# A max-pooling kernel with two input buffers: a half-length second load, and a shorter load near the end

## The chip, the core and the metric

The kernel runs on one core of one Trainium2 chip. Its time is the device time of one execution, in microseconds (us). Before the change the median of three runs is 335.14 us (334.92 to 335.22).

## What is computed

The input is a float32 array of 32 x 256 rows of 4096 numbers. Each row is cut into 256 windows of 16 numbers, and the output holds the maximum of each window:

```python
batch, channels, length = 32, 256, 4096
output_size = 256
...
for i in range(output_size):
    start = int(i * length / output_size)
    end = int((i + 1) * length / output_size)
    result[:, :, i] = np.max(x[:, :, start:end], axis=-1)
```

That is 134.2 MB read, 8.4 MB written, and one maximum over each 16 numbers.

## The kernel before

**Tiling.** All windows are spread over the 128 partitions, 16384 windows for each. A window takes 64 bytes of a partition, so a load of n windows brings n x 64 bytes into each partition as one row: 1024 windows are rows of 64 KB and 8 MB in all. The windows come in two groups, each laid out in memory as 128 long rows: group a with 13424 windows a partition, group b with 2960. Group a is walked from its end to its start, group b forwards.

**Loads.** The first load has 128 windows (8 KB rows), then come twelve of 1024, one of 1008, two of 1024, and a last one of 912. In this text the loads behind the first are named by the loop's counter, `n_loads` in the kernel before and `k` in the kernel after: k0, k1 and so on. Before the change, k0 to k11 have 1024 windows, k12 has 1008, k13 and k14 have 1024 and k15 has 912. All loads are issued by SyncE (SP) in this order, on one queue: L87 for the first, L96 for the rest. SP issues one after the other and waits at each until its buffer is free.

**Buffers.** One tile, `ring`, holds two buffers of 1024 + 152 windows. Even loads go to the lower, odd loads to the upper. Within its buffer a load lies at offset 0 or, for every second pair of loads (`moved`), at offset 152. VectorE (DVE) reduces every load in two instructions (L56): first the part that the next load in this buffer will overwrite (872 of 1024 windows), then the 152 windows that it won't touch. So load k+2 is issued as soon as the larger part of load k is reduced, beside the reduction of the smaller. The first load lies in the 152-window end of the lower buffer, and is out of the way of k0 and k1.

**Results.** They are collected in the tile `kept`. At the end the results of the last load, which lie in `ring`, are stored from ScalarE's queue (L114), and those of group a and of the rest of group b from SP's queue, behind the last load (L117).

Nothing else computes. TensorE, ScalarE and GpSimd have no work beyond that store and four constants.

Of the kernel before, what the change touches and what calls it, by code (L numbers as in the profile page):

```python
# [1 line left out]

# [4 lines left out]


@with_exitstack
def kernel(  # L10
    ctx: ExitStack,
    tc: tile.TileContext,
    x: bass.AP,
    output_size: bass.AP,
    out: bass.AP,
):

    nc = tc.nc
    P = nc.NUM_PARTITIONS
    fp32 = mybir.dt.float32

    B, C, L = x.shape
    O = int(output_size)  # L30
    assert L % O == 0, (L, O)
    W = L // O
    total = B * C * O // P
    assert B * C * O % P == 0

    CHUNK = 1024
    GAP = 152
    FIRST = 128
    LOADS_A, LOADS_B = 13, 2

    LESS = 16
    group_a = [FIRST] + [CHUNK] * (LOADS_A - 1) + [CHUNK - LESS]
    last = total - sum(group_a) - LOADS_B * CHUNK
    group_b = [CHUNK] * LOADS_B + [last]
    assert 0 < last and last * (W + 1) <= CHUNK * W

    pool = ctx.enter_context(tc.tile_pool(name="pool", bufs=1))
    ring = pool.tile([P, 2 * (CHUNK + GAP) * W], fp32, tag="ring", name="ring")
    kept = pool.tile([P, total - last], fp32, tag="kept", name="kept")

    xw = x.flatten_outer_dims().rearrange("r (o w) -> (r o) w", w=W)
    ow = out.flatten_outer_dims().rearrange("r o -> (r o)")

    def pooled(dst, at, n):

        nc.vector.reduce_max(  # L56
            out=dst,
            in_=ring[:, at * W : (at + n) * W].rearrange("p (n w) -> p n w", w=W),
            axis=mybir.AxisListType.X,
        )  # L60

    taken = 0

    def group(n):

        nonlocal taken
        span = slice(taken * P, (taken + n) * P)
        taken += n
        return (
            xw[span].rearrange("(p n) w -> p (n w)", p=P),  # L70
            ow[span].rearrange("(p n) -> p n", p=P),
        )

    stores = []
    n_loads = 0
    base = 0
    for g, loads in enumerate((group_a, group_b)):
        xg, og = group(sum(loads))
        a = sum(loads) if g == 0 else 0
        for n in loads:  # L80
            if g == 0:
                a -= n
            xn = xg[:, a * W : (a + n) * W]
            dst = kept[:, base + a : base + a + n] if n != last else None
            if n == FIRST:

                nc.sync.dma_start(  # L87
                    out=ring[:, CHUNK * W : (CHUNK + n) * W], in_=xn
                )
                pooled(dst, CHUNK, n)  # L90
            else:

                low = n_loads % 2 * (CHUNK + GAP)
                moved = n_loads // 2 % 2
                at = low + moved * GAP
                nc.sync.dma_start(out=ring[:, at * W : (at + n) * W], in_=xn)  # L96
                if n != last:
                    cut = CHUNK - GAP if moved else GAP
                    parts = [(0, cut), (cut, n)]
                    for u, v in parts if moved else parts[::-1]:  # L100
                        pooled(dst[:, u:v], at + u, v - u)
                else:
                    end = (at + CHUNK) * W
                    last_kept = ring[:, end - n : end]
                    pooled(last_kept, at, n)
                n_loads += 1
            if g:
                a += n
        full = a - last if g else sum(loads)
        stores.append((og[:, 0:full], kept[:, base : base + full]))  # L110
        base += full
    assert taken == total

    nc.scalar.dma_start(out=og[:, full : full + last], in_=last_kept)  # L114
    tc.no_sync_barrier()
    for dst, src in stores:
        nc.sync.dma_start(out=dst, in_=src)  # L117


# [1 line left out]
_INS = ['x', 'output_size']  # L121
_OUTS = [((32, 256, 256), 'float32')]

_NUMBERS = {'output_size': 256}


# [26 lines left out]
```

## Time and profile before

| | |
|---|---|
| median of three runs | 335.14 us (334.92 to 335.22) |
| span of the profiled execution, first to last instruction | 333.3 us |
| median above that span | 1.8 us |
| DVE busy | 276.6 us, 32 instructions |
| reduction of 872 windows | 14,686 ns each, 14 of them |
| reduction of 152 windows | 2676 ns each, 15 of them |
| reduction of the first load's 128 windows | 2286 ns |
| reduction of the last 912 windows | 15,353 ns |
| a full load, from issue to landing | 24.0 us, 14 of them in one median |
| first load of 1 MB, from issue to landing | 5.0 us |
| moved by DMA in all | 142.61 MB, 428 GB/s over the span |

The profile is that of one execution; what is known of its time is its span. The 1.8 us lie outside of first and last instruction. The profile's page gives the share of the span in which each engine is busy, the load on the DMA engines in 40 slices, the chain of work that ended last, and the costliest groups of instructions. In a table of stretches, each row is a stretch of time with the busy time of each engine, the granted TensorE clock (which nothing here uses), the mean busy share of the 16 DMA engines, and what they moved. DMA packets are booked at their end, so a stretch of a few us can show a share above 1. In the timeline a row is an instruction or a run of them: start, length, engine, line, and in brackets how long the engine had been idle and for what it waited. "SPq" is an instruction that issues a DMA.

### The profile page before, as it was taken

What the parts mean: (1) busy time and instruction counts of PE and PEld (TensorE: products, weight loads), DVE (VectorE), ACT (ScalarE), POOL (GpSimd) and SP (SyncE); (2) the same over time, 40 slices, a digit from 0 to 9 for tenths busy, and PEclk for the clock granted to TensorE, in tenths of its full rate; (3) what the DMA queues carried; (4) which work ended last, traced back from release to release, by engine and by line L of the source; (5) the groups of instructions that cost most, each with busy time, mean ns of one, the idle gap of its engine ahead of it and who ended that gap; (6) DMA issues with size and microseconds to landing.
All of it is one profiled execution on the core that took longest, in us unless ns stands there. A gap on an engine that the chain in (4) does not pass through costs nothing.

```text
span 333.3 us, 113 instructions
## 1 busy us (share of the span) xinstructions
DVE 276.6 (83%) x32; POOL 0.2 (0%) x4
## 2 busy tenths in 40 slices
DVE  2009979797997979799797979979797988979994
POOL 0000000000000000000000000000000000000000
DMA  9898989999898989999898989999898989899996
GB/s 377 377 503 377 503 377 488 393 425 456 377 503 377 503 377 488 393 448 433 377 503 377 503 377 488 393 456 425 389 480 381 495 377 503 377 462 448 421 412 285
DMA packets 2880, 142.61 MB, mean 428 GB/s; under 512 B 320, under 2 KB 320, under 8 KB 448
## 3 DMA queue, kind: packets, MB, share of 16 engines
q1 hardware_dynamic: 2736, 142.14, 98.7%
q10 hardware_dynamic: 144, 0.47, 0.3%
HBM read 134.22 MB, written 8.39 MB: 428 GB/s over the span
## 4 chain that ended last, share of the span: by engine, by line
DMA 57%; DVE 41%; issue 0%; SPq 0%
DMA ring<-in_x_dram 57%; DVE kept L56 36%; DVE ring L56 5%; SPq L87 0%
## 5 line engine op out<-in xcount | busy, mean ns | idle before, releaser
L56 DVE TENSOR_REDUCE kept<-ring 128x152 f32<-128x2432 f32 (+3 forms) x31 | 261.2, 8466 | 51.8 <-DMA ring<-in_x_dram 51.8
L56 DVE TENSOR_REDUCE ring<-ring 128x912 f32<-128x14592 f32 x1 | 15.4, 15353 | 0.1
L134 POOL MEMSET const-bfloat16-1.0<- 128x1 bf16 x1 | 0.1, 101 | 0.0
L134 POOL MEMSET const-uint8-127<- 128x1 uint8 x1 | 0.1, 101 | 0.0
L134 POOL MEMSET const-float32-0.0<- 128x1 f32 x1 | 0.1, 98 | 0.2 <-issue 0.2
L134 POOL MEMSET const-float32-1.0<- 128x1 f32 x1 | 0.1, 98 | 0.0
## 6 DMA issues: line engine op xcount, KB each, us to landing
ring<-in_x_dram SPq DMA_DIRECT2D x1, 8064.0 KB, 23.7
ring<-in_x_dram SPq DMA_DIRECT2D x1, 7296.0 KB, 21.9
out_dram<-kept SPq DMA_DIRECT2D x1, 6712.0 KB, 37.4
ring<-in_x_dram SPq DMA_DIRECT2D x1, 1024.0 KB, 5.0
out_dram<-kept SPq DMA_DIRECT2D x1, 1024.0 KB, 18.3
out_dram<-ring ACTq DMA_DIRECT2D x1, 456.0 KB, 4.0
ring<-in_x_dram SPq DMA_DIRECT2D x14, 24.0
```

The lines of the kernel that those rows point to most:

```text
L56: nc.vector.reduce_max(out=dst, in_=ring[:, at * W : (at + n) * W].rearrange("p (n w) -> p n w", w=W), axis=mybir.AxisListType.X,)
L134: nc = _bacc.Bacc("TRN2", target_bir_lowering=False, num_devices=1)
```

## The change

The load sizes become

```
before:  128,      12 x 1024, 1008, 2 x 1024, 912
after:   128, 512, 12 x 1024,  496, 2 x 1024, 912
```

A load of 512 windows (32 KB rows, 4 MB) goes between the first load and the first full one, and the load of 1008 windows becomes one of 496. The groups keep their sizes, and so do the stores. There is one load more: k0 has 512 windows, k1 to k12 have 1024, k13 has 496, k14 and k15 have 1024, k16 has 912. Each full load therefore stands one place later in the alternation of the buffers. The rule that sets buffer and offset is the same, and so is the rule that cuts a load into the two reductions: a load of 512 at offset 0 is cut into 360 and 152 windows, that of 496 into 344 and 152. On DVE two reductions are added (34 for 32). On SP one load is added, and no other instruction changes place.

The rest of the diff rewrites the same loop over a list of rows that is made first. Its core:

```diff
-    FIRST = 128
-    LOADS_A, LOADS_B = 13, 2
-    LESS = 16
-    group_a = [FIRST] + [CHUNK] * (LOADS_A - 1) + [CHUNK - LESS]
-    last = total - sum(group_a) - LOADS_B * CHUNK
-    group_b = [CHUNK] * LOADS_B + [last]
...
+    FIRST, SECOND = 128, 512
+    LESS = 16
+    RING = 2 * (CHUNK + GAP) * W
+    loads_a = [FIRST, SECOND] + [CHUNK] * 12 + [CHUNK - LESS - SECOND]
+    loads_b = [CHUNK] * 2
+    last = total - sum(loads_a) - sum(loads_b)
...
+    for k, (xg, a, n, dst) in enumerate(rows):
+
+        moved = k // 2 % 2
+        at = k % 2 * (CHUNK + GAP) + moved * GAP
+        nc.sync.dma_start(
+            out=ring[:, at * W : (at + n) * W], in_=xg[:, a * W : (a + n) * W]
+        )
+        if n != last:
+            cut = CHUNK - GAP if moved else GAP
+            assert cut < n
+            parts = [(0, cut), (cut, n)]
+            for u, v in parts if moved else parts[::-1]:
+                pooled(kept[:, dst + u : dst + v], at + u, v - u)
+        else:
+            end = (at + CHUNK) * W
+            last_kept = ring[:, end - n : end]
+            pooled(last_kept, at, n)
```

More of the change, by code (lines that the diff above doesn't have):

```diff
@@ L4 @@
 import concourse.tile as tile
-from concourse import bass_utils, mybir
+from concourse import mybir
 from concourse._compat import with_exitstack
@@ L34 @@
     assert B * C * O % P == 0
-    CHUNK = 1024
-    GAP = 152
-    FIRST = 128
-    LOADS_A, LOADS_B = 13, 2
-    LESS = 16
-    group_a = [FIRST] + [CHUNK] * (LOADS_A - 1) + [CHUNK - LESS]
-    last = total - sum(group_a) - LOADS_B * CHUNK
-    group_b = [CHUNK] * LOADS_B + [last]
[L45 to L49, printed above, removed]
     xw = x.flatten_outer_dims().rearrange("r (o w) -> (r o) w", w=W)
     ow = out.flatten_outer_dims().rearrange("r o -> (r o)")
[L54 to L60, printed above, removed]
     taken = 0
@@ L72, in group @@
         )
[L74 to L111, printed above, removed]
@@ L112 @@
-    assert taken == total
-    nc.scalar.dma_start(out=og[:, full : full + last], in_=last_kept)
+    CHUNK = 1024
+    GAP = 152
+    FIRST, SECOND = 128, 512
[4 more added lines that the diff above has]
+    last = total - sum(loads_a) - sum(loads_b)
+    assert 0 < last and last * (W + 1) <= CHUNK * W
+    pool = ctx.enter_context(tc.tile_pool(name="pool", bufs=1))
+    ring = pool.tile([P, RING], fp32, tag="ring", name="ring")
@@ new lines, with pooled @@
+    kept = pool.tile([P, total - last], fp32, tag="kept", name="kept")
+    def pooled(dst, at, n):
+        nc.vector.reduce_max(
+            out=dst,
+            in_=ring[:, at * W : (at + n) * W].rearrange("p (n w) -> p n w", w=W),
+            axis=mybir.AxisListType.X,
+        )
+    xa, oa = group(sum(loads_a))
+    xb, ob = group(sum(loads_b) + last)
+    assert taken == total
+    rows = []
+    a = sum(loads_a)
+    for n in loads_a:
+        a -= n
+        rows.append((xa, a, n, a))
@@ new lines @@
+    for n in loads_b + [last]:
+        rows.append((xb, a, n, sum(loads_a) + a))
+        a += n
+    xg, a, n, dst = rows.pop(0)
+    nc.sync.dma_start(
+        out=ring[:, CHUNK * W : (CHUNK + n) * W], in_=xg[:, a * W : (a + n) * W]
+    )
+    pooled(kept[:, dst : dst + n], CHUNK, n)
+    for k, (xg, a, n, dst) in enumerate(rows):
+        moved = k // 2 % 2
+        at = k % 2 * (CHUNK + GAP) + moved * GAP
+        nc.sync.dma_start(
+            out=ring[:, at * W : (at + n) * W], in_=xg[:, a * W : (a + n) * W]
+        )
+        if n != last:
[8 more added lines that the diff above has]
+            pooled(last_kept, at, n)
@@ L115 @@
+    full_b = sum(loads_b)
+    nc.scalar.dma_start(out=ob[:, full_b:], in_=last_kept)
     tc.no_sync_barrier()
-    for dst, src in stores:
-        nc.sync.dma_start(out=dst, in_=src)
+    nc.sync.dma_start(out=oa, in_=kept[:, : sum(loads_a)])
+    nc.sync.dma_start(out=ob[:, :full_b], in_=kept[:, sum(loads_a) :])
 _INS = ['x', 'output_size']
```

## The prediction, made before the changed kernel ran

> **What bounds the kernel now.** I read the page's first part, then the table of stretches, then the chain of waits in order of time, then the timeline. The page gives DVE as the only busy engine, and the chain that ended last as a mixture:
>
> ```profile
> span 333.3 us, 113 instructions
> ...
> DVE 276.6 (83%) x32; POOL 0.2 (0%) x4
> ...
> DMA 57%; DVE 41%; issue 0%; SPq 0%
> ```
>
> DVE is idle 17% of the span, so it is not the bound by itself. The chain has two readings. Either the DMA engines are full, or they idle while a load waits for its buffer, and the round trip (reduce, issue, load) sets the pace. The table of stretches decides; I cut it at DVE's starts, which are the landings (columns: stretch, length, DVE, POOL, clock, DMA share, GB/s):
>
> ```profile
> 5.79:25.11 19.32, 2.29 (x2) 0.00 (x0) 1.00 1.00 434
> 25.11:44.46 19.35, 17.28 (x3) 0.00 (x0) 1.00 1.00 434
> 237.98:257.03 19.05, 17.28 (x3) 0.00 (x0) 1.00 1.00 434
> 257.03:276.38 19.35, 17.01 (x3) 0.00 (x0) 1.00 1.00 434
> ```
>
> In the first row k0 and k1 are both queued from the start and nothing waits for a buffer. It takes 19.32 us for 1024 windows. In all later rows SP does wait for DVE, and the pace is the same, at a DMA share of 1.00. So **the DMA engines are the bound**, at 19.35 / 1024 = 18.90 ns a window, whether one load is queued or two. How thin the cover is, the chain shows:
>
> ```profile
> 218.63 14.70 DVE kept L56
> 233.33 0.02 issue
> 233.34 23.66 DMA ring<-in_x_dram
> 257.00 0.02 issue
> 257.03 14.43 DVE kept L56
> ```
>
> A load is issued 0.02 us after the larger part of load k-2 is reduced, and lands some 24 us later, of which 19.35 us are its own data. The other 4.6 us it stands behind the load before it. That is 19.35 (the neighbour's data) less 14.69 (the reduction) less 0.02: **while load k-2 is reduced, load k-1 must keep the DMA engines busy**, and a full one does so with 4.6 us to spare.
>
> **The change, part by part.** The times below are on the span's clock.
>
> *The 512-load at the start (k0).* The first load lands at 5.79. k0's data takes 512 x 18.90 ns = 9.68 us, so it lands at 15.47, where DVE now idles. Its larger part, 360 windows, takes 2.676 + 208 x (14.686 - 2.676)/720 = 6.15 us from the rows of 152 and 872, so k2 is issued at 21.6, 13 us before k1 lands (34.8). The queue is never empty, but it wasn't before: what goes is DVE's wait of 17.03 us, and it is split into one of 7.4 and one of about 10.5 us, with no byte arriving earlier. Value: **0**. From there each full load stands 9.68 us later than the one of the same k before, because the same windows have to arrive first; k12, the last full load of group a, lands at 237.98 + 9.68 = 247.66. k2 to k13 have a full neighbour in front of them, hence the same cover.
>
> *One more load and two more reductions.* SP's issue (0.33 us) lies in its wait. DVE's two instructions cost 2.676 - 152 x 16.68 ns = 0.14 us each beyond their windows; the 2.07 us that DVE waits before each load take them. Rows of 32 KB lie between those of 64 KB and of 8 KB. The first load's own 8 KB rows moved at the full pace once started, so 0; were they 1% slower, it would be 0.2 us for both half loads. The Trainium skill (page "DMA: Bandwidth & Descriptors", section "Where 436 GB/s comes from") says that HBM binds a load at about 358 GB/s; the 434 GB/s of the rows disagree, and the sum goes by the rows.
>
> *The short load near the end (k13, 496 windows).* It is the neighbour that must cover k12's reduction, and it holds only 496 x 18.90 ns = 9.37 us. k13 is issued early (k11's part is reduced at 243.0), follows k12 without a gap and lands at 257.03. k14 goes to k12's buffer, and is issued when k12's 872 windows are reduced: 247.66 + 14.69 + 0.02 = 262.37. So the queue is empty for 262.37 - 257.03 = **5.34 us**. In the kernel before, k12 with 1008 windows covered the same wait with 19.05 us.
>
> *Refilling the empty queue.* A load into an empty queue has a start and a landing that nothing hides. The trace has one such load, the first:
>
> ```profile
> 0.73 0.38 SPq L87 DMA_DIRECT2D ring<-in_x_dram  x1
> ...
> 5.79 2.29 DVE L56 TENSOR_REDUCE kept<-ring 128x128 f32<-128x2048 f32 x1 [5.79 <-DMA ring<-in_x_dram]
> ```
>
> From its issue to the landing are 5.06 us, of which 128 x 18.90 ns = 2.42 us are data: 2.64 us on top. Bounds: below, 0, if all of it could lie beside the end of k13; above, the store on ScalarE's queue, 4.0 us to landing with 456 KB (1.08 us at the pace) on the shared engines, so 2.9 us. A wider end is the whole 5.06 us. I take **2.64**, the row of the same kind. The Trainium skill (same page, section "Anatomy of one DMA") puts a fixed cost of about 2.0 us on one DMA; by that estimate the sum would be 0.6 us less, 342.5.
>
> So k14 lands at 262.37 + 2.64 + 19.35 = 284.36. The load with the same windows before it (k13 of the kernel before) landed at 276.38. The delay is **7.98 us**.
>
> *What it meets behind.* k15 is issued when the 344 windows of k13 are reduced. DVE is through with k12 at 264.9, the 344 take 5.88 us: 270.8, long before k14 lands. k15 has full cover and lands 19.35 us behind k14, k16 is issued 4.6 us before that, as the last load was before. DVE has 2.07 us to spare in each load but can't reduce what hasn't landed, and the DMA engines have nothing to spare. The tail is therefore shifted as a whole:
>
> ```profile
> 295.73 17.28 DVE L56 TENSOR_REDUCE kept<-ring 128x872 f32<-128x13952 f32 x2 [2.07 <-DMA ring<-in_x_dram]
> 313.06 15.35 DVE L56 TENSOR_REDUCE ring<-ring 128x912 f32<-128x14592 f32 x1
> 328.44 0.37 ACTq L114 DMA_DIRECT2D out_dram<-ring x1
> ```
>
> The stores from `kept` can't use the empty 8 us: they are issued behind the last load on SP's queue. **Sum:** 0 at the start, 0 for the added instructions, 5.34 + 2.64 = 7.98 near the end. Span 333.3 + 8.0 = 341.3. The median of the runs is 1.8 above the span of the profile, which I keep: 335.14 + 7.98 = **343.1 us**, 2.4% slower.
>
> **Rivals.**
>
> *Faster, by an earlier start (chance 0.03).* If the round trip and not the DMA engines set the pace, DVE's first long wait would be on the path. It would get its first large piece 9.68 us earlier, all its work would follow, and the gap near the end would be covered by loads that run ahead: 335.1 - 9.7 = 325.5, with 0.3 us for two instructions 325.8. It decides from the point where the engines can deliver over 434 GB/s with two loads queued. For it: the 57% and 41% of the chain, and 17.03 us of DVE idle. Against it: the row 5.79 to 25.11, where nothing is waited for and 434 GB/s is all there is. The Trainium skill ("Perfetto Trace Analysis", section "DMA Optimizations") says that splitting transfers lets some start sooner, which may shorten the whole if the DMA engines are generally idle; by its condition, and a share of 1.00, it brings nothing here.
>
> *No change (chance 0.03).* If k14 weren't held by k12's reduction, the queue would never be empty and everything would cancel: 335.1. Against it: k12 and k14 are both even and overlap in 872 windows of the lower buffer, and 14 loads of the trace waited in this way.
>
> *Half of it made up (chance 0.03).* If the end were DVE's, its idle 2.34 and 2.07 us before the last two full loads would be taken back: 343.1 - 4.4 = 338.7. Against it: the last load lands with DVE's end within 0.1 us, so a late load is a late end.
>
> *Slower still (chance 0.06).* If k14's wait counted one or both reductions of k13 as well, it would be issued at 270.8 or 273.5 instead of 262.4: 351.5 to 354.2. Against it: the trace of before issues right behind the larger part every time.
>
> *The forecast (chance 0.85)*, with the refill between its bounds: 335.14 + 5.34 = 340.5 to 335.14 + 5.34 + 2.9 = 343.4; the whole 5.06 us of refill would give 345.5. Of this last stretch I take in 1 us, to 344.4. **Range: 340.4 to 344.4.** It leaves out the rivals, which hold 0.15. A difference of 0.2% is about what a measurement of this kernel can tell from no change. Faster by over 0.2%: 0.03. Within: 0.03. Slower: 0.94.
>
> **What the changed profile would show.** The DMA share stays at 1.00 with 19.35 us a load until about 257 us, then about 8 us without landing data, the only hole before the end; DVE waits some 7 us at about 15 us, 10 at 25, and about 11 us (273.4 to 284.4) before the reduction of k14, which starts near 284.4. The last reduction is still 15.35 us and starts near 321. If k2 lands clearly before 54.1, my bound is wrong. If the hole is there and shorter than 5.3 us, my landing times are; if it is there and the end isn't 8 us late, the tail wasn't bound by the loads.

## The result, and the profile after

The changed kernel takes **343.76 us** (median of five runs, 343.58 to 344.04), before it was 335.14: a ratio of 1.0262, 95% interval 1.0251 to 1.0273, or 8.6 us slower. The forecast was 343.1. The profiled execution took 343.71 us with a span of 341.9, again 1.8 us apart.

The page after, the same three lines as before:

```profile
span 341.9 us, 118 instructions
...
DVE 276.7 (81%) x34; POOL 0.2 (0%) x4
...
DMA 62%; DVE 36%; issue 0%; SPq 0%; DVEq 0%
```

DVE does the same work, 276.7 us, in a longer span, and the share of the loads in the chain is larger. The timeline shows where, at the start and around the short load (start, length, engine, line; in brackets the wait before it):

```profile
5.66 2.29 DVE L57 TENSOR_REDUCE kept<-ring 128x128 f32<-128x2048 f32 x1 [5.66 <-DMA ring<-in_x_dram]
15.33 8.75 DVE L57 TENSOR_REDUCE kept<-ring 128x360 f32<-128x5760 f32 x2 [7.38 <-DMA ring<-in_x_dram]
34.68 17.28 DVE L57 TENSOR_REDUCE kept<-ring 128x872 f32<-128x13952 f32 x2 [10.61 <-DMA ring<-in_x_dram]
54.04 17.28 DVE L57 TENSOR_REDUCE kept<-ring 128x872 f32<-128x13952 f32 x2 [2.08 <-DMA ring<-in_x_dram]
...
247.54 25.66 DVE L57 TENSOR_REDUCE kept<-ring 128x872 f32<-128x13952 f32 x4 [2.08 <-DMA ring<-in_x_dram]
284.20 17.28 DVE L57 TENSOR_REDUCE kept<-ring 128x872 f32<-128x13952 f32 x2 [10.99 <-DMA ring<-in_x_dram]
...
303.55 17.28 DVE L57 TENSOR_REDUCE kept<-ring 128x872 f32<-128x13952 f32 x2 [2.07 <-DMA ring<-in_x_dram]
...
321.54 15.35 DVE L57 TENSOR_REDUCE ring<-ring 128x912 f32<-128x14592 f32 x1 [0.71 <-DMA ring<-in_x_dram]
```

DVE's one wait of 17.03 us at the start has become two, 7.38 and 10.61, and from 34.68 on the loads come every 19.35 us. At 247.54 DVE reduces k12 and k13 in one run of four instructions, and then waits 10.99 us for k14. The table of stretches shows the DMA engines in that time:

```profile
34.68:54.04 19.36, 17.28 (x3) 0.00 (x0) 1.00 1.00 433
...
247.54:257.00 9.46, 9.46 (x1) 0.00 (x0) 1.00 0.87 376
257.00:263.20 6.20, 6.20 (x2) 0.00 (x0) 1.00 0.00 0
```

The DMA share is 0.00 for 6.2 us, while DVE is busy all of that time. This is the load k14 waiting for the reduction of k12. The gap is longer than this row, because a packet is counted at its start and not at its end, as the text ahead of the prediction has it: the first packet of k14 takes 3.62 us and stands at 263.21, only 0.95 us after the issue; if that were its end, it would have begun before it was issued. A load moves as 128 rows, one for each partition, 16 at a time. In the packet records of the trace the last 16 rows of k13 end at 255.80 to 256.46, and the first 16 of k14 begin at 263.21 to 263.93, on average 7.3 us later. The chain of waits in order of time has the wait itself:

```profile
247.54 14.70 DVE kept L57
262.24 0.02 issue
262.26 21.92 DMA ring<-in_x_dram
284.18 0.02 issue
284.20 14.70 DVE kept L57
```

A load that took some 24 us from issue to landing before, 4.6 of them in the queue, here takes 21.92 us and has an empty queue before it. The last line of the timeline shows something new: before the last reduction DVE waits 0.71 us, where it was 0.04 us before the change.

### The profile page after: what moved, and what is told of

Its sections match the earlier page's. It is cut to its first block, busy times and chain, and to the rows that moved or that the text cites. A ratio compares the mean times of both kernels' runs of the same rounds, so it can differ in the third digit from the quotient of the medians.

```text
span 341.9 us, 118 instructions
## 1 busy us (share of the span) xinstructions
DVE 276.7 (81%) x34; POOL 0.2 (0%) x4
## 4 chain that ended last, share of the span: by engine, by line
DMA 62%; DVE 36%; issue 0%; SPq 0%; DVEq 0%
DMA ring<-in_x_dram 62%; DVE kept L57 32%; DVE ring L57 4%; SPq L78 0%; DVEq L57 0%
## 5 line engine op out<-in xcount | busy, mean ns | idle before, releaser
L57 DVE TENSOR_REDUCE kept<-ring 128x152 f32<-128x2432 f32 (+4 forms) x33 | 261.3, 7961 | 59.5 <-DMA ring<-in_x_dram 59.5
```

Of the source, the lines that this page charges most:

```text
L57: nc.vector.reduce_max(out=dst, in_=ring[:, at * W : (at + n) * W].rearrange("p (n w) -> p n w", w=W), axis=mybir.AxisListType.X,)
```

## The theories, and what tells them apart

My theory stands in the prediction. Rivals: half loads or one more load are dear in themselves; the early start is worth something that the hole hides; only truly empty time counts, without refill; the loss is one of total traffic, and goes if the hole is filled. A second question is the 0.6 us that came on top of the 8.0. All kernels below are the changed kernel with the edit shown ("..." marks lines left out); "before" was timed beside them at 335.0 to 335.1 us.

### Both half loads in front

```diff
-    loads_a = [FIRST, SECOND] + [CHUNK] * 12 + [CHUNK - LESS - SECOND]
+    loads_a = [FIRST, SECOND, CHUNK - LESS - SECOND] + [CHUNK] * 12
```

> The load of 496 windows moves from near the end to right behind that of 512, so both half loads stand at the start; nothing else changes. Theory (the short load costs only because it must cover the reduction of the full load before it): k1 of 496 windows need only cover the 360 windows of k0, 6.2 us, and its data takes 9.4 us, so the queue never runs empty, and there is no gain from the early start either: 335.1 to 335.4 us, with a share of 1.00 throughout. If the 0.6 us that came on top of the 8.0 us belong to the last load lying in the lower buffer, which it does here too, 335.8. Rival one (half loads are dear by themselves, wherever they stand): about 343.8, as after the change. Rival two (the earlier start of DVE is worth something that the hole near the end hid): under 334.5.

Measured: 336.02 us, ratio 1.0030 (1.0018 to 1.0041). The same sizes in another order take 7.7 us less, so half loads are not dear by themselves. But it is 1.0 us above before, more than the theory said. Its timeline shows the place:

```profile
24.82 8.48 DVE L57 TENSOR_REDUCE kept<-ring 128x344 f32<-128x5504 f32 x2 [0.67 <-DMA ring<-in_x_dram]
...
44.94 17.28 DVE L57 TENSOR_REDUCE kept<-ring 128x872 f32<-128x13952 f32 x2 [11.64 <-DMA ring<-in_x_dram]
```

k2 comes 20.12 us behind k1 instead of 19.35: 0.77 us late, though it was issued some 3.2 us before k1 landed. The rest is another load, k7, which comes 0.24 us late though it was issued 4.6 us before k6 landed; the reason stays open. So it wasn't the last load's place in the lower buffer, as my expectation had it: the last load comes 17.24 us behind k15 here, as in the kernel before.

The same with more cover, 384 and 624 windows:

```diff
-    FIRST, SECOND = 128, 512
+    FIRST, SECOND = 128, 384
...
-    loads_a = [FIRST, SECOND] + [CHUNK] * 12 + [CHUNK - LESS - SECOND]
+    loads_a = [FIRST, SECOND, CHUNK - LESS - SECOND] + [CHUNK] * 12
```

> Both smaller loads in front as in the kernel with 512 and 496, but as 384 and 624 windows. There k2 was issued 3.2 us before k1 landed and came 0.77 us late. Here k0's 232 windows are reduced at about 17 us and k1 lands at about 24.7, so 7.8 us are left. Theory (a load has to be issued some 2.7 to 4 us before the queue runs empty; beyond that the order of the sizes is of no account): k2 lands 19.35 us behind k1, and the time is that of before, 335.0 to 335.3 us. Rival (one more load, or the last load in the lower buffer, costs something by itself): 335.6 to 336. Rival (earlier start gains): under 334.5.

Measured: 335.19 us, ratio 1.0004 (0.9996 to 1.0013), no difference.

```profile
5.66 2.29 DVE L57 TENSOR_REDUCE kept<-ring 128x128 f32<-128x2048 f32 x1 [5.66 <-DMA ring<-in_x_dram]
12.93 6.61 DVE L57 TENSOR_REDUCE kept<-ring 128x232 f32<-128x3712 f32 x2 [4.98 <-DMA ring<-in_x_dram]
24.75 10.61 DVE L57 TENSOR_REDUCE kept<-ring 128x472 f32<-128x7552 f32 x2 [5.21 <-DMA ring<-in_x_dram]
44.10 17.28 DVE L57 TENSOR_REDUCE kept<-ring 128x872 f32<-128x13952 f32 x2 [8.74 <-DMA ring<-in_x_dram]
...
312.99 15.35 DVE L57 TENSOR_REDUCE ring<-ring 128x912 f32<-128x14592 f32 x1
```

k2 comes 19.35 us behind k1, and the last reduction starts at 312.99, where it was 313.06 before. Neither the additional load and its two reductions nor the last load's buffer costs anything that this measurement can tell, and DVE's earlier start (at 12.93 instead of 25.11) brings nothing. Of the versions that read all windows it is the best, and it is not better than the kernel before.

### Each half of the change alone

At the start only:

```diff
-    loads_a = [FIRST, SECOND] + [CHUNK] * 12 + [CHUNK - LESS - SECOND]
+    loads_a = [FIRST, SECOND] + [CHUNK] * 11 + [CHUNK - LESS]
...
-    last = total - sum(loads_a) - sum(loads_b)
+    last = total - 512 - sum(loads_a) - sum(loads_b)
...
```

> The load of 512 windows at the start alone: the load near the end has 1008 windows again, and one of the twelve full loads is left out. 512 windows of each partition are neither read nor stored, so the output is incomplete. Theory (the early start is worth nothing, since the DMA engines are full either way): the kernel before, less 512 x 18.90 ns = 9.68 us of loading and 0.60 us of storing (0.26 MB at 434 GB/s): 324.9 us. Rival (the early start is worth something): clearly less than 324.5. If the last load is 0.6 us late again although it lies in the upper buffer as before the change, and there is no hole: 325.5.

Near the end only:

```diff
-    loads_a = [FIRST, SECOND] + [CHUNK] * 12 + [CHUNK - LESS - SECOND]
+    loads_a = [FIRST] + [CHUNK] * 12 + [CHUNK - LESS - SECOND]
...
-    last = total - sum(loads_a) - sum(loads_b)
+    last = total - 512 - sum(loads_a) - sum(loads_b)
...
```

> The short load of 496 windows near the end alone: there is no load of 512 at the start. 512 windows of each partition are neither read nor stored, so the output is incomplete. Number of loads and places of the buffers are those of the kernel before (the last load in the upper buffer). Theory (the hole is due to the short load alone): before, less 9.68 us of loading and 0.60 us of storing, plus 7.9 us of hole as the profile after shows it: 332.7 us. The last load came 0.67 us late after the change, and 0.77 and 1.08 us late with 752 and 848 windows, but not with both half loads in front. If this goes with the hole, 333.4 and the last rows of the last load slow again; if it goes with the place in the lower buffer, 332.7 and no slow rows. Rival (the hole needs the early start at the front): 324.8.

Measured: 324.73 and 333.54 us (ratios 0.9694, 0.9681 to 0.9708, and 0.9957, 0.9945 to 0.9970). Against 335.05 less 10.28 us for the windows left out, 324.8, the start alone is worth nothing, and the end alone costs 8.8 us, the whole loss. The short load needs no help from the front. The hole is 8.2 us here (274.88 less 237.94, 9.37 and 19.35). The end alone also has the late last load, though it lies in the upper buffer:

```profile
274.88 17.28 DVE L57 TENSOR_REDUCE kept<-ring 128x872 f32<-128x13952 f32 x2 [11.28 <-DMA ring<-in_x_dram]
...
294.23 17.28 DVE L57 TENSOR_REDUCE kept<-ring 128x872 f32<-128x13952 f32 x2 [2.07 <-DMA ring<-in_x_dram]
...
312.69 15.35 DVE L57 TENSOR_REDUCE ring<-ring 128x912 f32<-128x14592 f32 x1 [1.18 <-DMA ring<-in_x_dram]
```

### The size of the short load

```diff
-    FIRST, SECOND = 128, 512
+    FIRST, SECOND = 128, 256
```

> The load at the start has 256 windows instead of 512, and the short one near the end 752 instead of 496. Theory (a load must cover 14.71 us of reduction and issue and 2.64 us of refill, 17.35 us in all, and what its data lacks of that is lost): 752 x 18.90 ns = 14.21 us, so 3.1 us are lost: 338.3 us, or 338.9 with the 0.6 us that came on top after the change. Rival (only the time in which the queue is really empty is lost, and the refill lies beside the end of the load before): 14.71 - 14.21 = 0.5 us: 335.6, or 336.2.

The other has 160 in this place:

> 160 windows at the start, 848 near the end. Theory (17.35 us to be covered): 848 x 18.90 ns = 16.03 us, 1.3 us lost: 336.5 us, or 337.1 with the 0.6 us on top. Rival (only empty time counts): nothing lost, 335.1, or 335.7.

Measured: 339.14 us (ratio 1.0124, 1.0110 to 1.0137) and 337.35 us (1.0067, 1.0053 to 1.0081). The rival without refill (335.6 to 336.2, and 335.1 to 335.7) is out. The first two lines are of the kernel with 752 windows, the others of that with 848; "SPq" in each is the issue of k14 and of the loads behind it:

```profile
257.58 36.97 SPq L87 DMA_DIRECT2D ring<-in_x_dram  x3
279.51 17.28 DVE L57 TENSOR_REDUCE kept<-ring 128x872 f32<-128x13952 f32 x2 [6.71 <-DMA ring<-in_x_dram]
...
255.46 37.11 SPq L87 DMA_DIRECT2D ring<-in_x_dram  x3
277.53 17.28 DVE L57 TENSOR_REDUCE kept<-ring 128x872 f32<-128x13952 f32 x2 [5.25 <-DMA ring<-in_x_dram]
```

The reduction of k14 starts at 279.51 and at 277.53; k12's start (242.86 and 240.75), the short load's data and 19.35 us would give 276.42 and 276.13. That is 3.09 and 1.40 us late, where 3.14 and 1.32 were expected. From its issue (257.58 and 255.46) k14 takes 19.35 us and 2.58 or 2.72 us on top, and after the change 2.59. So in these three kernels k14 lands at its issue + 2.6 + its data. This holds even with 848 windows, where k14 was issued 1.3 us before k13 landed. The DMA engines had still run out of rows: in the packet records k13's last rows end at 255.91 to 256.45 and k14's first begin at 256.43 to 257.02, on average 0.5 us later, and those first rows take 2.83 to 3.57 us instead of the usual 2.42. A load that is issued early enough lands behind the load before it, by the time of its own data. The edge between the two is not sharp: k2 with 512 and 496 windows was issued 3.2 us ahead and still came 0.77 us late, with no pause between the rows. The rest, 0.9 to 1.0 us each, is the late last load again.

### The short load in the middle

```diff
-    loads_a = [FIRST, SECOND] + [CHUNK] * 12 + [CHUNK - LESS - SECOND]
+    loads_a = [FIRST, SECOND] + [CHUNK] * 4 + [CHUNK - LESS - SECOND] + [CHUNK] * 8
```

> After the change, but the load of 496 windows stands in the middle, as k5 behind three or four full ones (k0 has 512, k1 to k4 have 1024), and full loads take the places up to k14. Theory (a short load costs wherever it follows a full one, because it has to cover that one's reduction): the hole of 7.9 us appears between k5 and k6, around 105 us of the span, and the time is that of after, 343.0 to 343.8 us. Rival (the loads behind the hole catch up, if there are enough of them): less, down to 335.1. It also tells whether the slow last rows of the last load belong to a hole near by or to any hole before them: if to any, the last load lands some 18 us behind k15 and the time is 343.7; if to a near one, 17.25 us and 343.0.

Measured: 343.70 us, ratio 1.0255 (1.0241 to 1.0269), the time of after.

```profile
92.94 25.66 DVE L57 TENSOR_REDUCE kept<-ring 128x872 f32<-128x13952 f32 x4 [2.08 <-DMA ring<-in_x_dram]
130.11 17.28 DVE L57 TENSOR_REDUCE kept<-ring 128x872 f32<-128x13952 f32 x2 [11.51 <-DMA ring<-in_x_dram]
149.43 17.28 DVE L57 TENSOR_REDUCE kept<-ring 128x872 f32<-128x13952 f32 x2 [2.03 <-DMA ring<-in_x_dram]
```

The hole has moved to 110 us with the short load, and nine full loads behind it at 19.35 us each recover nothing. It is a little larger here: 130.11 less 92.94, 9.37 and 19.35 gives 8.45 us against 7.94 after the change (284.20 less 247.54, 9.37 and 19.35). The last load is only 0.1 us late (17.36 us behind k15), so of the two readings in the expectation the near hole fits better. That the total is that of after the change all the same is a coincidence of these two parts. Why the hole is larger here stays open.

### A store in the hole

```diff
+    LOW, HIGH = 2 * CHUNK - LESS - SECOND, 8304
...
             pooled(last_kept, at, n)
+        if k == 13:
+            tc.no_sync_barrier()
+            nc.sync.dma_start(out=oa[:, LOW:HIGH], in_=kept[:, LOW:HIGH])
+            tc.no_sync_barrier()
...
-    nc.sync.dma_start(out=oa, in_=kept[:, : sum(loads_a)])
+    nc.sync.dma_start(out=oa[:, :LOW], in_=kept[:, :LOW])
+    nc.sync.dma_start(out=oa[:, HIGH:], in_=kept[:, HIGH : sum(loads_a)])
```

> After the change, but 6784 windows of the results of group a (3.5 MB, 8.0 us at 434 GB/s) are stored in a DMA of their own, issued on SP's queue between the short load and the load behind it, at about 245.5 us of the span, when the smaller part of k11 is reduced; so it fills the hole. The rest of group a is stored at the end in two pieces. Theory (after the hole the loads set the end, since 15.4 us of reduction and the store of the last results follow the last load): the hole is gone from the DMA share, k14 lands at 284.2 to 284.6 as after the change, and the time stays at 343 to 343.8 us; only the last store has an empty queue and can land up to 0.5 us earlier. Rival (the end is set by the sum of all transfers, so that the hole is lost only as long as nothing fills it): 8 us less, 335.4 to 336.

Measured: 344.23 us, ratio 1.0271 (1.0257 to 1.0285), against 343.76 after the change. The hole is filled, and the time is none the better:

```profile
257.00:263.20 6.20, 6.20 (x2) 0.00 (x0) 1.00 0.97 420
```

The DMA share in the stretch that was empty is 0.97, and in the packet records k14's first rows follow the store's last ones 0.1 us later on average. My expectation missed one thing: k14 starts to be reduced at 285.96, 1.4 us later than I gave it room for. It was issued about 3 us before the store in front of it had landed, and is again not quite covered, like k2 with 512 and 496 windows. What the store in the hole saves lies behind the last reduction: from its end to the end of the span it is 5.0 us after the change and 3.6 us here, not the 0.5 us that I had put on it. This speaks against the total traffic: 8 us of stores taken out of the end are worth 1.4 us there, because the end hangs on the last load and its 15.35 us of reduction. The last load is late here too, though nothing was left of the hole:

```profile
305.30 17.28 DVE L58 TENSOR_REDUCE kept<-ring 128x872 f32<-128x13952 f32 x2 [2.06 <-DMA ring<-in_x_dram]
...
323.49 15.35 DVE L58 TENSOR_REDUCE ring<-ring 128x912 f32<-128x14592 f32 x1 [0.91 <-DMA ring<-in_x_dram]
```

### Nothing queued behind the last load

```diff
-    nc.sync.dma_start(out=oa, in_=kept[:, : sum(loads_a)])
     nc.sync.dma_start(out=ob[:, :full_b], in_=kept[:, sum(loads_a) :])
+    tc.no_sync_barrier()
+    nc.sync.dma_start(out=oa, in_=kept[:, : sum(loads_a)])
```

> After the change, but of the two stores from kept the small one of group b, which has to wait for the reduction of k15, is issued ahead of the large one of group a. So nothing is queued behind the last load while it runs. It is to show why the last rows of the last load take 0.5 to 1.3 us longer than their neighbours. If the store queued behind them does this, the rows are fast, the last load lands 17.25 us behind k15, and the reduction of the last load starts 0.6 us earlier; the stores begin some 2.6 us later, with an empty queue, so the time is 343.7 + 2 = 345 to 346.5 us. If it does not, the last rows are slow again, and the last load lands 17.9 us behind k15.

Measured: 344.58 us, ratio 1.0287 (1.0272 to 1.0303); less than the 345 to 346.5 expected. The last reduction starts 0.72 us earlier than after the change, and from its end to the end of the span it is 6.5 us instead of 5.0:

```profile
303.52 17.28 DVE L57 TENSOR_REDUCE kept<-ring 128x872 f32<-128x13952 f32 x2 [2.06 <-DMA ring<-in_x_dram]
...
320.82 15.35 DVE L57 TENSOR_REDUCE ring<-ring 128x912 f32<-128x14592 f32 x1
```

The last reduction starts at 320.82 with no wait. In the packet records no row of the last load is slow. After the change its last 16 rows, and only those, take 0.45 to 1.3 us longer than the usual 2.15 us. So the store queued behind the last load makes it late. It doesn't do so in every kernel. The extra time of the slowest last row is 0.2 us in the kernel before, 0.25 with 384 and 624 windows, and 0.4 us with the start alone and with both half loads in front, all with the same store behind them and without a hole. It is 1.4 us with 752 windows, with 848 and with the end alone, and 0.6 us with the hole far in front. The hole itself is not what these kernels share. With 848 windows the pause is only 0.5 us, and the last load is 1.1 us late, more than the 0.7 us behind the pause of 7.3 us after the change. With the store in the hole there is no pause; the last rows are 0.1 to 0.9 us slower, some of the first too, by up to 1.4 us, and the last load lands 18.11 us behind k15, 0.9 us late. In all kernels with a last load that was clearly late, the load two places before it had been late. A late load far in front (k2 with both half loads in front, k6 with the short load in the middle) left the last one on time or 0.1 us late. Why that should matter stays open.

## Why the prediction was right, and where it was off

**The bound** was read rightly: the loads keep 19.35 us with a share of 1.00 wherever they are covered, however early DVE starts. The row 5.79 to 25.11, where nothing waits for a buffer, had decided it.

**The load at the start, 0:** right. The start alone came out at 324.73, within 0.2 us of before less its windows.

**The hole, 5.34 + 2.64 = 7.98 us:** right. k14's reduction started at 284.20 instead of 284.36; against the other loads of the same execution it was 7.94 us late. In the packet records this is a pause of 7.3 us and, on top, first rows of k14 that take 2.96 to 3.62 us instead of 2.42. The refill was 2.6 to 2.7 us in three kernels, 2.5 with the stores swapped, 2.9 with the end alone and 3.1 with the hole in the middle. The first load, off which 2.64 was read, gives 2.2 to 2.7 us in the eleven traces. So the size is right, and its agreement to 0.05 us with the changed kernel is luck. The fixed cost of about 2.0 us in the Trainium skill ("DMA: Bandwidth & Descriptors", section "Anatomy of one DMA") is below each of these refills; the runs decide for 2.6. That section is on DMAs issued from GpSimd; these loads are issued from SP. The lower end that I had kept for the refill, 0, is refuted by the two sizes.

**"The tail is therefore shifted as a whole":** this step put the last load's part at nothing, and it was 0.7 us. The last load landed 17.92 us behind k15 instead of 17.25, and because DVE's end and this landing had fallen together before, all of it went to the end. 7.94 and 0.67 make the 8.6 us that were measured. The swapped stores show that the store behind the load is needed for it; what else is needed stays open, since it also came with the hole filled. That the range still holds the time is luck: the refill within its bounds gave at most 343.4, and 343.76 lies in the last 1 us of the range, which was taken in for a longer refill and not for a late last load.

**The rivals:** the earlier start gained nothing (both kernels with the half loads in front); the loads caught nothing up (the hole in the middle); and k14 waited for the larger part of k12 alone (issued at 262.26, forecast 262.37).

## What to carry to other kernels

With two buffers and full DMA engines, a load has a second task: its transfer covers the time in which the other buffer is freed. Before shortening one, compare its transfer time with that reduction plus the refill of the queue, here 14.7 + 2.6 us, and leave some 2 us more (loads issued 4.3 us ahead were on time); what it lacks is lost for good, since full engines have no way to catch up (nine full loads recovered nothing here). An engine's long wait at the start is worth nothing while the resource it waits for is already full.

## What the runs showed that I had not expected

The edge of the cover isn't sharp. The last load apart, a load issued 4.3 us or more before the one ahead of it landed came 0.25 us late at most; at 3.2 us (both halves in front) it came 0.8 us late, and behind a store with 3 us 1.3 us late. In both, a few of the first 16 rows were up to 1 us slow, among them the one that began last (at 24.40 with 3.25 us, and at 265.37 with 3.31 us, instead of 2.42), and a load has landed only when all its rows have. Between 3.2 and 4.3 us nothing was measured. And a load that came late had an effect far behind it: the last 16 rows of the last load, some 55 us after the hole, ran 0.45 to 1.3 us slower, if a store was queued behind them.
